# A gated block on one core: the last gate rows of adaLN placed one behind every second weight chunk of both down sweeps

## The chip, the cores and the metric

One of the cores of a Trainium2 chip runs the whole kernel. The metric is the device time of one execution in microseconds (us), as the median of several runs. The engines are named as in the profile: PE is TensorE (matmul), PEld its weight loads, DVE is VectorE, ACT is ScalarE, POOL is GpSimd, SP is SyncE, which here issues the DMAs from one queue, in order. A wait of SP before it issues a DMA is shown under SPq.

## The reference, cut to what matters

One decoder block over 512 tokens of width 2048, in float32. A vector `c` sets six modulation vectors of width 2048 (shift, scale and gate of both sub-layers). The change concerns the last of them, `gt2`, which is the gate of the gated MLP:

```
c_act = silu(c)
mod = c_act @ w_ada + b_ada                 # 2048 -> 6 * 2048
sh1, sc1, gt1, sh2, sc2, gt2 = split(mod, 6)
...
x = x + gt2 * (act @ w_down)                # act: 512 x 5632, w_down: 5632 x 2048
return rmsnorm(x) * norm_f_g
```

## The kernel before, in words

The kernel is one long program for all engines, written in Python and ordered by a scheduler at build time. The scheduler simulates the engines and picks, at each step, the earliest instruction in program order whose operands and buffers are ready in its simulation; the order in which it picks them is the order of each engine's queue. On the chip each engine runs its queue in that order and waits on semaphores. A buffer group (a tag with so many `bufs`) hands out its buffers in turn, so an instruction that fills a buffer waits until the readers of its former content are done.

Activations lie transposed: 128 channels on the partitions, 512 tokens along the row. Each float32 matmul is made as three: weights and activations are split into a high part (`hi`, rounded) and a low part (`lo`, the rest), and `mm3` (lines 120 to 123) issues hi*hi, hi*lo and lo*hi. A weight chunk is 128 x 512 float32, 256 KB, four tiles of 128 x 128. `split_weights` (lines 110 to 118) loads it (`wraw`, 4 buffers), rounds it on ACT (`whi`, 3 buffers, line 115) and subtracts on DVE (`wlo`, 3 buffers, line 117). So one chunk makes 12 matmuls. `project` (lines 125 to 135) runs over the chunks of one output tile.

The last stage is the product with `w_down`, from line 1050 on. The 44 activation tiles were stored to DRAM by the stage before (`actd`). `act_tiles` (lines 1061 to 1067) loads four of them, a slab, through the same four `wraw` buffers (under the name `ald`) and splits each on ACT and DVE (lines 143 and 144). Sweep 1 (lines 1088 to 1101) computes output tiles 0 to 7: 11 slabs, and in each slab one chunk for each of the 8 output tiles, summed up in 8 PSUM banks: 88 chunks. In its last slab `residual` (lines 806 to 809) multiplies each finished bank by its gate, adds it to `x2` and adds the square to `acc`. Sweep 2 (lines 1104 to 1109) does the same for output tiles 8 to 15 over the first 9 slabs: 72 chunks. A tail (lines 1110 to 1126) takes the last two slabs of these tiles in two halves of the tokens, and then normalises and stores the output. The 16 `x2` tiles are loaded at the start of the stage (line 1054).

The gate needs 16 x 128 sums over 2048 products each, and those are made on DVE: `ada_gate2` (lines 1079 to 1085) takes a quarter `kq` of the 2048 inputs, loads that quarter of `c_act` broadcast over the partitions (`cb`, 2 buffers, line 1081), and for each output tile `j` loads a row of weights, 128 x 512 float32, 256 KB (`wa`, 2 buffers, line 1084), and multiplies and sums it in one DVE instruction into `modg` (line 1085). There are 4 x 16 = 64 such rows. They are called in sweep 1, at the head of slabs 1 to 8, eight rows at a time; in slab 9 four small additions on `modg` (lines 1094 to 1097) form the gate `mod[:, 80:96]`, which `gate(f)` (line 1058) hands to the residuals. Nothing ties a row to a place in the sweep but its data, its buffers and its place in program order.

Of the kernel before, what the change touches and what calls it, by code (L numbers as in the profile page):

```python
# [1 line left out]

# [1 line left out]

# [5 lines left out]
F32 = mybir.dt.float32  # L10
# [3 lines left out]
ALU = mybir.AluOpType  # L14
PSUM = bass.MemoryType.PSUM

P = 128
T = 512
D = 2048
KT = D // P  # L20
NF = 44
# [7 lines left out]
NB = 8  # L29
# [5 lines left out]
DK = 4  # L35
# [27 lines left out]
def block_kernel(ctx, tc, a, out, stop=None, dbg=None):  # L63
    nc = tc.nc
    V, S, G, PE = nc.vector, nc.scalar, nc.gpsimd, nc.tensor
# [23 lines left out]
    def cols(name, lo, hi):  # L89
        return vec[:, COLS[name] + lo : COLS[name] + hi]  # L90
# [11 lines left out]
    mod = cp.tile([P, 96], F32, tag="mod", name="mod")  # L102
# [3 lines left out]
    V.tensor_scalar_add(b1p, cols("b_ada", 16, 32), 1.0)  # L106

    mark = [None, None]

    def split_weights(src, eng=V):  # L110
        w = src.shape[-1]
        raw = wp.tile([P, WC], F32, tag="wraw", name="wraw", bufs=4)
        nc.sync.dma_start(raw[:, 0:w], src)
        hi = wp.tile([P, WC], F32R, tag="whi", name="whi", bufs=3)
        mark[0] = S.copy(hi[:, 0:w], raw[:, 0:w]).ins  # L115
        lo = wp.tile([P, WC], F32R, tag="wlo", name="wlo", bufs=3)
        mark[1] = eng.tensor_tensor(lo[:, 0:w], raw[:, 0:w], hi[:, 0:w].bitcast(F32), op=ALU.subtract).ins  # L117
        return hi, lo

    def mm3(ps, wh, wl, xh, xl, start, stop):  # L120
        PE.matmul(ps, wh, xh, start=start, stop=False)  # L121
        PE.matmul(ps, wh, xl, start=False, stop=False)  # L122
        return PE.matmul(ps, wl, xh, start=False, stop=stop)  # L123

    def project(ps, src, acts, start=True, stop=True, engs=(V,)):

        n = len(acts)
        for k0 in range(0, n, WC // P):
            nk = min(WC // P, n - k0)
            wh, wl = split_weights(src[:, k0 * P : (k0 + nk) * P], engs[k0 // 4 % len(engs)])  # L130
            for kk in range(nk):
                k = k0 + kk
                sl = slice(kk * P, (kk + 1) * P)
                last = mm3(ps, wh[:, sl], wl[:, sl], *acts[k], start=start and k == 0, stop=stop and k == n - 1)
        return last

    def slots(k, tag="a"):
        return (actp.tile([P, T], F32R, tag=f"{tag}h{k}", name=f"{tag}h{k}"),
                actp.tile([P, T], F32R, tag=f"{tag}l{k}", name=f"{tag}l{k}"))
# [32 lines left out]
    cact = tc.dram_tile([1, D], F32, name="cact")  # L172
# [6 lines left out]
    if True:  # L179
        cb = p0.tile([P, D], F32, tag="cb", name="cb")  # L180
# [29 lines left out]
        for k in range(KT):  # L210
# [7 lines left out]
            hi, lo = slots(k)  # L218
# [15 lines left out]
        S.copy(rstd, psb)  # L234
        pu.append(pf_bank(7))
        project(pu[7], a["winu7"], H1)
        for i in range(8):
            t = p0.tile([P, T], F32, tag="us", name="us", bufs=2)
# [6 lines left out]
        for k in range(KT):  # L245
# [3 lines left out]
            hi, lo = slots(k)  # L249
# [94 lines left out]
    def win_tile(fi):  # L344
        ps = mmtile()
        project(ps, a["win1"][fi - 8, :, :], H)
        return ps
# [354 lines left out]
    def load_cells(g, names):  # L702
        got = []
        for i in names:
            t = cell(RKV[i], RKV[i].lower())
            for x in range(2):
                nc.sync.dma_start(two(t)[:, x, :], sp[2 * g + x, i])
            got.append(t)
        return got
# [5 lines left out]
    for g in range(NQ):  # L715
# [9 lines left out]
        if g < NQ - 1:  # L725
            win_some(pairs, (0, 2))
            with tc.high_priority(offset=50000):
                r, k = load_cells(g + 1, (0, 1))
# [29 lines left out]
    for f in range(NW):  # L758
        if f % 2 == 0:
            xt = two(cell("K" if f % 4 == 0 else "R", "xt"))  # L760
            nc.sync.dma_start(xt, a["xT"][:, f : f + 2, :])
        ps = mmtile()
        project(ps, a["wout"][f, :, 0 : NM * P], M)
        V.scalar_tensor_tensor(xt[:, f % 2, :], ps, mod[:, 32 + f : 33 + f], xt[:, f % 2, :], op0=ALU.mult, op1=ALU.add)
        d = tc.dram_tile([P, T], F32, name=f"part{f}")
        nc.sync.dma_start(d, xt[:, f % 2, :])
        part.append(d)
# [11 lines left out]
    rb = ctx.enter_context(tc.tile_pool(name="rb", bufs=1, reuse_waits="tile"))  # L779
# [26 lines left out]
    def residual(f, ps, gate, acc, lo, hi, fresh):  # L806

        V.scalar_tensor_tensor(x2[f][:, lo:hi], ps, gate, x2[f][:, lo:hi], op0=ALU.mult, op1=ALU.add)
        sumsq(acc, x2[f][:, lo:hi], lo, hi, fresh)
# [122 lines left out]
    for j in range(2, NORD):  # L932
        tiles = []
        for i in range(2):
            ps = bank()
            last = project(ps, a["wup"][2 * j + i - 4, :, :], H2)
# [78 lines left out]
    for n in range(NST):  # L1015
# [12 lines left out]
        t1, t2, t3, t4 = ([TK[k][i] for k in ks] for i in range(4))  # L1028
# [29 lines left out]
    def gate(f):  # L1058
        return mod[:, 80 + f : 81 + f]

    def act_tiles(k0):
        got = []
        for k in range(k0, k0 + DK):
            t = wp.tile([P, WC], F32, tag="wraw", name="ald", bufs=4)
            nc.sync.dma_start(t, actd[k])
            got.append(split_act(k % KT, t))
        return got

    def down(ps, f, k0, n, acts, start, stop):
        project(ps, a["wdn"][f, :, k0 * P : (k0 + n) * P], acts, start=start, stop=stop)  # L1070
# [5 lines left out]

    modg = cp.tile([P, 4, KT], F32, tag="modg", name="modg")

    def ada_gate2(kq, js):
        cb = rb.tile([P, T], F32, tag="t0", name="cb2", bufs=2)  # L1080
        nc.sync.dma_start(cb, cact[0:1, kq * T : (kq + 1) * T].partition_broadcast(P))
        for j in js:
            wa = rb.tile([P, T], F32, tag="t1", name="wa3", bufs=2)
            nc.sync.dma_start(wa, a["ada3"][kq, j, :, :])
            V.scalar_tensor_tensor(wa, wa, 1.0, cb, op0=ALU.mult, op1=ALU.mult, accum_out=modg[:, kq, j : j + 1])  # L1085

    pss = [bank() for _ in range(NB)]
    for k0 in range(0, NF, DK):
        A = act_tiles(k0)
        n = k0 // DK  # L1090
        if 1 <= n <= 8:
            ada_gate2((n - 1) // 2, range(8 * ((n - 1) % 2), 8 * ((n - 1) % 2) + 8))
        if n == 9:
            V.tensor_add(modg[:, 0, :], modg[:, 0, :], modg[:, 1, :])
            V.tensor_add(modg[:, 2, :], modg[:, 2, :], modg[:, 3, :])
            V.tensor_add(modg[:, 0, :], modg[:, 0, :], modg[:, 2, :])
            V.tensor_add(mod[:, 80:96], modg[:, 0, :], cols("b_ada", 80, 96))
        for f in range(NB):
            down(pss[f], f, k0, DK, A, k0 == 0, k0 + DK == NF)
            if k0 + DK == NF:  # L1100
                residual(f, pss[f], gate(f), acc, 0, T, f == 0)
    pss = [bank() for _ in range(NB)]
    KL = NF - 2 * DK
    for k0 in range(0, KL, DK):
        A = act_tiles(k0)
        for f in range(NB):
            down(pss[f], NB + f, k0, DK, A, k0 == 0, k0 + DK == KL)
            if k0 + DK == KL:
                V.scalar_tensor_tensor(x2[NB + f], pss[f], gate(NB + f), x2[NB + f], op0=ALU.mult, op1=ALU.add)
    A = act_tiles(KL) + act_tiles(KL + DK)  # L1110
    for hf in range(2):
        for n in range(NB):
            f = NB + n
# [121 lines left out]
```

## Time and profile before

| | us |
|---|---|
| median of 3 runs | 2365.94 |
| the three runs | 2362.83, 2365.94, 2372.0 |
| time of the profiled execution | 2367.17 |
| its span, first to last instruction | 2365.4 |
| first matmul of sweep 1 | 1836.8 |
| first and last gate row (starts) | 1860.7, 2004.6 |

All places in time are us from the start of the span. A group's line in the profile gives, after the bar, its busy time, the mean ns of one instruction, and the idle time of the engine just before them with what ended it. A matmul's duration is modelled and overlaps the next one's; where matmuls follow each other without a pause, their starts are 0.227 us apart in this stage. The granted clock of PE (`PEclk`) is 1.00 at full speed.

### The profile page before, as it was taken

How to read it: one execution, taken by the hardware profiler on the slowest of the kernel's cores; microseconds unless marked ns; L12 is line 12 of the kernel's file. 1: busy time of each engine (PE TensorE's matmuls, PEld its weight loads, DVE VectorE, ACT ScalarE, POOL GpSimd, SP SyncE). 2: the span in 40 equal slices, each digit the busy share in tenths (PEclk: the TensorE clock that was granted, in tenths of full speed). 3: DMA queues.
4: the chain of work that ended last, by engine and by line, in shares of the span. 5: the costliest groups of instructions: out<-in, count | busy, mean ns of one | idle time of the engine just before them, and what ended most of it. 6: DMA issues, size and time to landing. Idle time of an engine off the chain costs nothing.

```text
span 2365.4 us, 41904 instructions
## 1 busy us (share of the span) xinstructions
PE 2224.0 (94%) x16306; PEld 1883.8 (80%) x16306; DVE 1512.8 (64%) x2532; ACT 924.0 (39%) x1551; POOL 404.7 (17%) x390
## 2 busy tenths in 40 slices
PE   7998888898979899999999999999999998999997
PEld 5776656665656798889999999999999766888886
DVE  7897667576876469766566666665666555353357
ACT  4335233242423255544434444444444322343333
POOL 0000000000000005643443343433342000000000
PEclk9999999999989999999999999999999999999998
DMA  9885555636775575533333333333334877555555
GB/s 349 301 305 170 157 188 164 205 117 206 226 225 163 179 225 169 148 115 109 116 121 115 113 121 108 116 116 113 109 115 133 272 242 231 148 152 143 143 164 179
DMA packets 197466, 401.42 MB, mean 170 GB/s; under 512 B 37521, under 2 KB 49553, under 8 KB 193041
## 3 DMA queue, kind: packets, MB, share of 16 engines
q1 hardware_dynamic: 197266, 398.73, 53.1%
q8 instruction: 128, 2.10, 0.4%
q14 instruction: 72, 0.59, 0.1%
HBM read 364.56 MB, written 34.09 MB: 169 GB/s over the span
## 4 chain that ended last, share of the span: by engine, by line
PE 48%; DMA 5%; DVE 2%; issue 1%; ACT 0%; SPq 0%; DVEq 0%; ACTq 0%
PE b L123 16%; PE b L121 16%; PE b L122 16%; DMA wa<-ada 2%; DMA ald<-actd 2%; DMA wraw<-wdn 1%; DVE wlo L117 1%; DVE wa L1085 0%; DVE x L1074 0%; DMA x<-x2d 0%; ACT ah L143 0%; DVE al L144 0%; ACT whi L115 0%; SPq L1054 0%; PE b L170 0%
## 5 line engine op out<-in xcount | busy, mean ns | idle before, releaser
L115 ACT CAST whi<-wraw 128x512 fp32r<-128x512 f32 (+1 forms) x594 | 360.1, 609 | 827.8 <-DMA wraw<-wup 264.6
L117 DVE TENSOR_TENSOR wlo<-wraw,whi 128x512 fp32r<-128x512 f32 (+1 forms) x578 | 406.0, 705 | 248.3 <-ACT whi L115 239.9
L123 PE MATMUL b<-ah,wlo 128*128 128x512 f32 (+1 forms) x980 | 352.6, 360 | 16.9 <-DVE wlo L117 15.9
L121 PE MATMUL b<-ah,whi 128*128 128x512 f32 (+1 forms) x980 | 351.3, 358 | 9.4 <-ACT whi L115 8.4
L122 PE MATMUL b<-al,whi 128*128 128x512 f32 (+1 forms) x980 | 349.5, 357 | 0.0
L123 PE MATMUL b<-hh,wlo 128*128 128x512 f32 (+1 forms) x640 | 237.4, 371 | 5.5 <-DVE wlo L117 5.4
L121 PE MATMUL b<-hh,whi 128*128 128x512 f32 (+1 forms) x640 | 237.7, 371 | 0.0
L122 PE MATMUL b<-hl,whi 128*128 128x512 f32 (+1 forms) x640 | 237.2, 371 | 0.0
L123 PEld LDWEIGHTS b<-ah,wlo 128*128 128x128 f32 x980 | 186.6, 190 | 53.2 <-DVE wlo L117 26.6
L121 PEld LDWEIGHTS b<-ah,whi 128*128 128x128 f32 x980 | 186.6, 190 | 38.6 <-ACT whi L115 13.7
L122 PEld LDWEIGHTS b<-al,whi 128*128 128x128 f32 x980 | 186.5, 190 | 26.4
L969 DVE TENSOR_TENSOR pl<-raw,ph 128x768 fp32r<-128x768 f32 x104 | 102.9, 989 | 153.6 <-ACT ph L968 153.6
L123 PE MATMUL mm<-ah,wlo 128*128 128x512 f32 x444 | 186.6, 421 | 6.6 <-DVE wlo L117 6.6
L121 PE MATMUL mm<-ah,whi 128*128 128x512 f32 x444 | 185.5, 418 | 7.2 <-ACT whi L115 6.6
L122 PE MATMUL mm<-al,whi 128*128 128x512 f32 x444 | 183.8, 414 | 0.0
L957 POOL TENSOR_TENSOR sums<-sums,raw 128x256 f32<-128x256 f32 x104 | 107.6, 1034 | 416.1 <-DVE sl L969 410.2
L123 PE MATMUL b<-tk,sl 128*128 128x256 f32 x624 | 176.7, 283 | 0.5 <-DVE sl L969 0.5
L122 PE MATMUL b<-tk,sh 128*128 128x256 f32 x624 | 176.6, 283 | 0.0
L121 PE MATMUL b<-tk,sh 128*128 128x256 f32 x624 | 176.1, 282 | 0.0
L372 DVE SCALAR_TENSOR_TENSOR war<-war,cq 128x1024 f32<-128x1024 f32 x96 | 117.2, 1222 | 85.5 <-DMA war<-ada 85.1
L968 ACT CAST ph<-raw 128x768 fp32r<-128x768 f32 x104 | 86.4, 831 | 164.4 <-PE b L122 157.8
L956 POOL TENSOR_TENSOR sums<-raw 128x512 f32<-128x512 f32 x104 | 137.7, 1324 | 67.9 <-DMA raw<-wups 36.3
(277 smaller groups left out, 4711.1 us busy)
## 6 DMA issues: line engine op xcount, KB each, us to landing
raw<-wups SPq DMA_DIRECT2D x104, 512.0 KB, 3.5
war<-ada SPq DMA_DIRECT2D x96, 512.0 KB, 4.3
wraw<-wdn SPq DMA_DIRECT2D x192, 256.0 KB, 3.1
wraw<-wup SPq DMA_DIRECT2D x160, 256.0 KB, 3.6
wa<-ada SPq DMA_DIRECT2D x32, 1024.0 KB, 7.7
wraw<-win SPq DMA_DIRECT2D x108, 256.0 KB, 4.1
ald<-actd SPq DMA_DIRECT2D x88, 256.0 KB, 2.8
wraw<-wout SPq DMA_DIRECT2D x78, 256.0 KB, 4.0
```

The source lines that it names most:

```text
L115: mark[0] = S.copy(hi[:, 0:w], raw[:, 0:w]).ins
L117: mark[1] = eng.tensor_tensor(lo[:, 0:w], raw[:, 0:w], hi[:, 0:w].bitcast(F32), op=ALU.subtract).ins
L121: PE.matmul(ps, wh, xh, start=start, stop=False)
L122: PE.matmul(ps, wh, xl, start=False, stop=False)
L123: return PE.matmul(ps, wl, xh, start=False, stop=stop)
L372: V.scalar_tensor_tensor(wa, wa, 1.0, cq[0], op0=ALU.mult, op1=ALU.mult, accum_out=modq[:, kq, j : j + 1])
L956: G.tensor_tensor(sa, raw[:, 1:3, :], raw[:, 0:1, :].to_broadcast([P, 2, W2]), op=ALU.add)
L957: G.tensor_tensor(sb2[:, 0, :], sa[:, 0, :], raw[:, 2, :], op=ALU.add)
L968: act = S.copy(hi[:, sl, :], t)
L969: dve = V.tensor_tensor(lo[:, sl, :], t, hi[:, sl, :].bitcast(F32), op=ALU.subtract)
```

## The change

`ada_gate2` becomes a generator. It yields a row when the load of the row after it has been traced too, so that loads are traced one row ahead. Two generators are chained: one makes output tiles 0 to 7 over the four quarters (32 rows), the other tiles 8 to 15 (32 rows); at the seam the second starts its loads only when its first row is asked for. Broadcasts stay at eight in all, rows at 64.

`project` now records the last matmul of each chunk in `beats`. `gate_step(n)` is called after each chunk of both sweeps with the chunk's number, 0 to 87 in sweep 1 and 88 to 159 in sweep 2. On every second chunk from 6 on it takes the next row and gives its DVE instruction an ordering edge behind the last matmul of that chunk (`in_step`). The edge is of the class `NoSync`: the scheduler keeps the order, and no semaphore is waited for on the chip. The loads of rows have no such edge. The first 32 rows end at chunk 68, the last at chunk 132; behind each, four additions half as wide as before form the gate of that half. The first residual that needs a gate comes after chunk 80, the first that needs the second half after chunk 152.

```
+    def in_step(op, beat):
+        tc.add_manual_dep(op.ins, beat.name, mybir.DependencyInfo(mybir.DependencyClass.NoSync,
+                                                                  mybir.DependencyReason.DATA), reason="pace")
...
                 last = mm3(ps, wh[:, sl], wl[:, sl], *acts[k], start=start and k == 0, stop=stop and k == n - 1)
+            beats.append(last.ins)
         return last
...
-    def ada_gate2(kq, js):
-        cb = rb.tile([P, T], F32, tag="t0", name="cb2", bufs=2)
-        nc.sync.dma_start(cb, cact[0:1, kq * T : (kq + 1) * T].partition_broadcast(P))
-        for j in js:
-            wa = rb.tile([P, T], F32, tag="t1", name="wa3", bufs=2)
-            nc.sync.dma_start(wa, a["ada3"][kq, j, :, :])
-            V.scalar_tensor_tensor(wa, wa, 1.0, cb, op0=ALU.mult, op1=ALU.mult, accum_out=modg[:, kq, j : j + 1])
+    def ada_gate2(js):
+        loaded = []
+        for kq in range(4):
+            cb = rb.tile([P, T], F32, tag="t0", name="cb2", bufs=2)
+            nc.sync.dma_start(cb, cact[0:1, kq * T : (kq + 1) * T].partition_broadcast(P))
+            for j in js:
+                wa = rb.tile([P, T], F32, tag="t1", name="wa3", bufs=2)
+                nc.sync.dma_start(wa, a["ada3"][kq, j, :, :])
+                loaded.append((wa, cb, modg[:, kq, j : j + 1]))
+                if len(loaded) == 2:
+                    yield loaded.pop(0)
+        yield loaded.pop(0)
+
+    rows = itertools.chain(ada_gate2(range(NB)), ada_gate2(range(NB, KT)))
+
+    def gate_step(n):
+        if n % 2 or n < 6:
+            return
+        row = next(rows, None)
+        if row:
+            wa, cb, got = row
+            in_step(V.scalar_tensor_tensor(wa, wa, 1.0, cb, op0=ALU.mult, op1=ALU.mult, accum_out=got), beats[-1])
+        done = (n - 4) // 2
+        if done in (4 * NB, 4 * KT):
+            lo = done // 4 - NB
+            r = slice(lo, lo + NB)
+            V.tensor_add(modg[:, 0, r], modg[:, 0, r], modg[:, 1, r])
+            V.tensor_add(modg[:, 2, r], modg[:, 2, r], modg[:, 3, r])
+            V.tensor_add(modg[:, 0, r], modg[:, 0, r], modg[:, 2, r])
+            V.tensor_add(mod[:, 80 + lo : 80 + lo + NB], modg[:, 0, r], cols("b_ada", 80 + lo, 80 + lo + NB))
...
         A = act_tiles(k0)
-        n = k0 // DK
-        if 1 <= n <= 8:
-            ada_gate2((n - 1) // 2, range(8 * ((n - 1) % 2), 8 * ((n - 1) % 2) + 8))
-        if n == 9:
-            V.tensor_add(modg[:, 0, :], modg[:, 0, :], modg[:, 1, :])
-            V.tensor_add(modg[:, 2, :], modg[:, 2, :], modg[:, 3, :])
-            V.tensor_add(modg[:, 0, :], modg[:, 0, :], modg[:, 2, :])
-            V.tensor_add(mod[:, 80:96], modg[:, 0, :], cols("b_ada", 80, 96))
         for f in range(NB):
             down(pss[f], f, k0, DK, A, k0 == 0, k0 + DK == NF)
+            gate_step(k0 // DK * NB + f)
...
             down(pss[f], NB + f, k0, DK, A, k0 == 0, k0 + DK == KL)
+            gate_step((NF + k0) // DK * NB + f)
```

More of the change, by code (lines that the diff above doesn't have):

```diff
@@ L1 @@
 from contextlib import ExitStack
+import itertools
 import numpy as np
@@ L108, in block_kernel @@
     mark = [None, None]
+    beats = []
+    def in_step(op, beat):
+        tc.add_manual_dep(op.ins, beat.name, mybir.DependencyInfo(mybir.DependencyClass.NoSync,
+                                                                  mybir.DependencyReason.DATA), reason="pace")
     def split_weights(src, eng=V):
```

## The prediction

> **What bounds the kernel now.** I read the page first, to see whether TensorE is the limit, and then only the stretch that the edit touches, the two down sweeps: equal amounts of matmul work compared (the windows view), who waited for whom (the waits view), the chain of waits, and single instructions (the timeline).
>
> ```profile
> span 2365.4 us, 41904 instructions
> PE 2224.0 (94%) x16306; PEld 1883.8 (80%) x16306; DVE 1512.8 (64%) x2532; ACT 924.0 (39%) x1551; POOL 404.7 (17%) x390
> ```
>
> PE looks busy nearly everywhere, so gains can only sit in a stage where it stands still. One chunk of weights feeds 12 matmuls. The two stretches below each hold 50 chunks, that is 600 matmuls (the count in brackets has one or two more that straddle an edge). The first is chunks 7 to 56 of sweep 1, with the 64 gate rows; the second is the next 50 chunks, without any row.
>
> ```profile
> core 0: us, PE busy (x) PEld busy (x) DVE busy (x) ACT busy (x) POOL busy (x), PEclk, DMA share, GB/s
> 1860.72:2018.59 157.87, 143.68 (x601) 110.57 (x600) 91.48 (x208) 45.40 (x76) 0.00 (x0) 1.00 0.76 242
> 2018.59:2154.67 136.08, 136.08 (x602) 112.73 (x601) 60.16 (x89) 50.20 (x83) 0.00 (x0) 1.00 0.51 145
> ```
>
> The reader is to see three things. The same work takes 157.87 us with the rows and 136.08 without: **21.8 us are lost while the rows run**, at a full granted clock in both. A clean chunk takes 136.08 / 50 = 2.72 us, and PE is busy for every microsecond of the clean stretch, so 2.72 us is the floor. And the core's DMA engines carry 242 GB/s at a share of 0.76 there, busy but not full.
>
> Only 14.2 us of the loss (157.87 - 143.68) show as PE idle. The Trainium skill ("Perfetto Trace Analysis", Identifying the Most-Contended Engine) says that matmul busy share is a poor measure, since matmuls are pipelined, and wants the LDWEIGHTS share. The rows agree that it understates: matmul busy time alone would make the sum 7.6 us smaller. I go by equal counts of matmuls, which need neither.
>
> Who stopped PE in the first stretch, then what DVE and SP waited for there:
>
> ```profile
> PE b L123 <- DVE wlo L117: 11.5, 15, 1.5
> PE b L121 <- ACT whi L115: 2.5, 4, 1.0
> DVE wa L1085 <- DMA wa<-ada: 45.1, 38, 3.5
> SPq L1084 <- DVE wa L1085: 57.4, 57, 3.1
> SPq L1065 <- DVE mod L1097: 5.0, 1, 5.0
> by line: DMA wa<-ada 36.1%; DMA ald<-actd 21.6%; issue 9.6%; DVE wa L1085 6.9%; DVE wlo L117 5.3%; PE b L123 4.2%; PE b L121 3.6%; PE b L122 3.6%; DMA wraw<-wdn 2.7%; ACT ah L143 2.0%; DVE al L144 1.8%; SPq L1084 0.7%; SPq L113 0.6%; ACT wh
> ```
>
> The last line is the chain of waits for that stretch: it runs through the loads of the rows, not through PE. Columns of the others are total, times, longest. PE waits 19 times, 14.0 us, for a chunk's split. DVE waits 45.1 us for row loads with the splits queued behind; SP waits 57.4 us to issue a row's load until DVE has freed one of two buffers, with weight loads queued behind. One instance:
>
> ```profile
> 1923.25 0.69 DVE L1085 SCALAR_TENSOR_TENSOR wa<-wa,cb 128x512 f32<-128x512 f32 x1 [0.90 <-DMA wa<-ada]
> ...
> 1924.68 0.69 DVE L1085 SCALAR_TENSOR_TENSOR wa<-wa,cb 128x512 f32<-128x512 f32 x1 [0.73 <-DMA wa<-ada]
> ...
> 1925.30 0.69 DVE L117 TENSOR_TENSOR wlo<-wraw,whi 128x512 fp32r<-128x512 f32 x1
> 1926.04 0.50 PE L123 MATMUL b<-ah,wlo 128*128 128x512 f32 x1 [0.62 <-DVE wlo L117]
> ```
>
> Two rows each wait for their load, the split stands behind them, and PE's idle ends when the split does.
>
> **The change, part by part.** *The pace of the rows.* Before, the rows run as fast as two buffers let them:
>
> ```profile
> L1085 DVE SCALAR_TENSOR_TENSOR wa<-wa,cb x64: 681/691/695, 1860.7 to 2004.6; 128x512 f32<-128x512 f32 x64
> L1085 DVE DVE_READ_ACCUMULATOR wa<-wa,cb x64: 78/81/83, 1861.4 to 2005.2; 128x1 f32 x64
> wa<-ada SPq DMA_DIRECT2D x62, 256.0 KB, 3.6
> cb<-cact SPq DMA_DIRECT2D x7, 256.0 KB, 4.7
> ```
>
> 64 rows lie between 1860.7 and 2004.6, one every 143.9 / 63 = 2.28 us. A buffer's round is its load, 3.6 us, and the row, 0.69 + 0.08 = 0.77 us: 4.37 us, and with two buffers one row per 2.19 us. So the rows sit on the latency of their own loads. After, one row stands behind every second chunk: a row per 2 x 2.72 = 5.44 us. Its load can be issued once the row two before it is done, 10.9 us earlier; 3.6 us after that it has landed, some 7 us ahead of need. Neither DVE nor SP should wait for rows, and the 21.8 us go. That the second half of the rows has its buffers traced only at its first row changes little, since a load that waits for nothing but a buffer needs no beat.
>
> *What the rows still cost DVE.* Until row 64 (chunk 132) each chunk pair has a row of 0.77 us more: 14% of 5.44 us on top of 60.16 / 136.08 = 44%. The cover is the lead of the splits over PE in the clean stretch:
>
> ```profile
> 2068.18 0.69 DVE L117 TENSOR_TENSOR wlo<-wraw,whi 128x512 fp32r<-128x512 f32 x1 [2.03 <-ACT whi L115]
> 2072.99 0.39 PE L121 MATMUL b<-ah,whi 128*128 128x512 f32 x1
> ACT whi L115 <- PE b L122: 121.2, 69, 2.1
> ```
>
> The split at 2068.18 is that of the chunk which PE begins at 2072.99: 4.8 us ahead, with 2.03 us of DVE idle before it, because ACT is held by PE (121.2 us over the clean rest of the sweeps): the split buffers are full. A row of 0.77 us fits in the idle and costs nothing; without that cover it would cost 64 x 0.77 = 49 us.
>
> *The stretch where DVE is fullest*, the last slab of sweep 1 with its eight residuals, now gets four rows:
>
> ```profile
> 2083.87:2105.63 21.76, 21.76 (x97) 18.02 (x96) 17.75 (x27) 12.01 (x21) 0.00 (x0) 1.00 0.52 145
> ```
>
> DVE goes from 17.75 to 17.75 + 4 x 0.77 = 20.8 of 21.76 us. It still fits: from nothing to 4 x 0.77 = 3.1 us, and I take nothing, as the row above shows PE without a pause and the lead of 4.8 us stands behind it. Below nothing is out, PE being at its floor.
>
> *SP and the slab starts.* Queued behind a row's load on SP are weight and activation loads. At a slab start the lead is thinnest:
>
> ```profile
> 2051.14 7.21 SPq L113 DMA_DIRECT2D wraw<-wdn  x6
> 2059.39 0.39 PE L121 MATMUL b<-ah,whi 128*128 128x512 f32 x1
> wraw<-wdn SPq DMA_DIRECT2D x98, 256.0 KB, 2.9
> ald<-actd SPq DMA_DIRECT2D x49, 256.0 KB, 2.7
> L115 ACT CAST whi<-wraw 128x512 fp32r<-128x512 f32 (+1 forms) x594 | 360.1, 609 | 827.8 <-DMA wraw<-wup 264.6
> ```
>
> The slab's first weight load leaves at 2051.14, 8.2 us before PE needs it; landing takes 2.9 us, ACT 0.6 and DVE 0.7, which leaves some 4 us. A row's load and a row in between take perhaps 1 us. 16 slab starts have rows about them (chunks 8 to 128). Bounds: nothing (the clean slabs pause nowhere) to the mean pause of before, 14.0 / 19 = 0.74 us, each: 0 to 11.9 us. I take 1.2 us, near the clean rows, because traffic stays under that of before: per slab of 21.8 us twelve loads of 256 KB become 16.5 (four rows, half a broadcast), 145 x 16.5 / 12 = 199 GB/s against 242.
>
> *The start of sweep 1.* The first broadcast and two rows are now traced ahead of slab 1's activations:
>
> ```profile
> 1847.22 1.64 SPq L113 DMA_DIRECT2D wraw<-wdn  x3
> 1849.82 0.33 SPq L1081 DMA_DIRECT2D cb<-cact  x1
> 1853.25 0.50 PE L121 MATMUL b<-ah,whi 128*128 128x512 f32 x1 [2.66 <-ACT whi L115]
> 1836.80:1860.72 23.92, 21.26 (x85) 16.78 (x84) 8.80 (x13) 7.37 (x12) 0.00 (x0) 0.93 0.90 293
> ```
>
> PE idles 2.66 us here for the weights issued at 1847.22, while the x2 tiles load. That pause stays. Three loads of 256 KB ahead of those weights would lengthen it by 0.79 MB / 293 GB/s = 2.7 us; the broadcast away from beside them would shorten it by 0.9 us. I take +0.6, as the weights of chunks 5 and 6 still stand ahead of the rows.
>
> *The small sums.* Four additions become eight of half the width, twice four:
>
> ```profile
> 2005.56 0.17 DVE L1096 TENSOR_TENSOR modg<-modg 128x16 f32<-128x16 f32 x1
> ```
>
> 0.17 us each, in DVE's idle: nothing. The 5.0 us that SP waited behind them lie in the 21.8. Bytes, rows and broadcasts (8) stay as many.
>
> **Sum.** -21.8 + 1.2 + 0.6 = -20.0 us. The profiled execution took 2367.17 us, its span 2365.4 and 1.8 around it; it becomes 2347.2. The median of the three runs, 2365.94, lies 1.2 below it and becomes **2345.9 us**. With all the loss recovered and 0.9 at the start it would be 2343.2.
>
> **The rivals.** *Two buffers still bind.* The Trainium skill ("Perfetto Trace Analysis", Optimization Strategy) reads the same gap repeating on the engine that should be saturated as a sign of too few buffers; by that rule alone the loss would stay, for the change adds none. As a mechanism here: if a row's load leaves less than 3.6 us before its row, because it stands on SP behind weight loads that wait for their own buffers, DVE still waits in front of the splits. Against it: 5.44 us per row is 2.5 times the two-buffer floor of 2.19. If half of the rows meet it, half the loss stays: 2365.9 - 10.9 = 2355.0 us.
>
> *The edge does not hold the rows.* It orders by schedule and adds no wait on the chip; if the scheduler fulfils it early, rows bunch as before: 2365.9 us.
>
> *Slower: SP holds the weights up.* A row's load now waits on SP for a row that stands behind PE-paced splits; everything after it in SP's one queue waits too. Its place is the slab start, with 4 us to spare; from a hold of more than 4 us each row passes it on to PE. Before, a row cost PE 21.8 / 64 = 0.34 us, which is the point of no gain. At the mean pause of 0.74 us per row the loss is 64 x 0.74 = 47.4 us, and the time 2365.9 - 21.8 + 47.4 = 2391.5 us. For it: SP's 57.4 us of such waits now. Against it: the weight load behind waits for the next split anyway, which DVE does right after the row.
>
> **How the numbers follow.** About 0.5% (12 us) is what a measurement of this kernel can tell from no change, so faster means under 2354.1 us. Forecast 0.73; two buffers bind 0.12; the edge does not hold 0.09; SP holds the weights 0.06. Half of the second lies under 2354.1: faster 0.73 + 0.06 = 0.79; same 0.06 + 0.09 = 0.15; slower 0.06. The range runs from 2341 (2343.2, less about 2 us for the run: the fastest of the three lies 3.1 below their median) to 2358, which takes in the second case and the unknown costs at 13.8 instead of 1.8 us, over two thirds of their bounds (11.9 + 2.7 + 3.1 = 17.7); it leaves out the last two cases, 0.15, and a little of the others.
>
> **What would show it.** Right: the sixty-four rows spread over 126 chunks, about 343 us, from near 1858 to near 2200; no DVE wait for row loads worth the name; SP's wait at line 1084 may stay, as nothing behind it is urgent; PE's waits in the sweeps fall from 14.0 us to under 2; 50 chunks from chunk 7 on take 136 to 138 us. Wrong: rows still 2.3 us apart; PE waiting for splits at slab starts; the pause before chunk 5 grown by more than 3 us; PE pauses in sweep 2, which has none now.

## The result, and the profile after

| | before | after |
|---|---|---|
| median of 6 runs each, us | 2367.79 | 2345.81 |
| range of the runs | 2362.83 to 2372.0 | 2339.4 to 2351.19 |
| time of the profiled execution, us | 2367.17 | 2346.13 |
| its span, us | 2365.4 | 2344.4 |
| first matmul of sweep 1 to the end of the span, us | 528.6 | 506.6 |

The ratio of after to before is 0.9903 (95% interval 0.9882 to 0.9925): faster by 22.0 us, or about 1%. In the code after the change the row's product is line 1108, its load 1094, its broadcast 1091; the split of weights is line 124 on DVE and 122 on ACT, the matmuls are lines 128 to 130, the loads of weights 120 and of activations 1073.

First the windows view of the two stretches of 50 chunks that the prediction compared, chunks 7 to 56 and the 50 behind them:

```profile
core 0: us, PE busy (x) PEld busy (x) DVE busy (x) ACT busy (x) POOL busy (x), PEclk, DMA share, GB/s
1861.68:1997.68 136.00, 136.00 (x601) 112.65 (x600) 66.99 (x127) 46.21 (x77) 0.00 (x0) 1.00 0.67 203
1997.68:2133.70 136.02, 136.02 (x602) 112.66 (x601) 75.58 (x143) 50.34 (x83) 0.00 (x0) 1.00 0.66 198
```

The first stretch took 157.87 us before; it takes 136.00, 2.72 us per chunk, and PE is busy through all of it. The second, which had no rows before and has them now, takes 136.02 us against 136.08. So 21.9 us went where the rows had been, and nothing was paid where the rows went. The rows' line (durations in ns, first and last start):

```profile
L1108 DVE SCALAR_TENSOR_TENSOR wa<-wa,cb x64: 682/685/689, 1859.1 to 2204.3; 128x512 f32<-128x512 f32 x64
```

Who waited for whom (total, times, longest): DVE from 1861 to 2230 us, then SP in the first stretch. The same view of PE has no line at all.

```profile
DVE wlo L124 <- ACT whi L122: 146.1, 107, 2.0
DVE al L152 <- ACT ah L151: 29.7, 48, 1.9
DVE x L816 <- PE b L130: 2.4, 2, 1.4
DVE acc L812 <- ACT sqx L811: 1.0, 4, 0.5
```

```profile
SPq L120 <- DVE wlo L124: 37.1, 30, 2.3
...
SPq L1094 <- DVE wa L1108: 5.2, 22, 0.3
```

The rows lie (2204.3 - 1859.1) / 63 = 5.48 us apart, 2.28 before. DVE's 45.1 us of waits for row loads are all gone. SP still waits for row buffers, 22 times in the stretch, but at most 0.3 us at a time. In the timeline of DVE a row now follows a split at once and the next split still comes early:

```profile
1925.22 0.69 DVE L124 TENSOR_TENSOR wlo<-wraw,whi 128x512 fp32r<-128x512 f32 x1 [0.95 <-ACT whi L122]
1925.83 0.68 DVE L1108 SCALAR_TENSOR_TENSOR wa<-wa,cb 128x512 f32<-128x512 f32 x1
1926.44 0.08 DVE L1108 DVE_READ_ACCUMULATOR wa<-wa,cb 128x1 f32 x1
1927.71 0.69 DVE L124 TENSOR_TENSOR wlo<-wraw,whi 128x512 fp32r<-128x512 f32 x1 [1.19 <-ACT whi L122]
```

The split behind the row waits 1.19 us for ACT, so the row sat in time that was idle anyway.

The spans differ by 21.0 us, the stage by 22.0. The difference lies ahead of the change: sweep 1 starts at 1836.8 before and 1837.8 after, and the change does not touch the code up to there. Over all the profiles of this study that start lies between 1832.0 and 1843.4 us, and both ends come from one and the same kernel (the last experiment): a spread of 11.4 us, about as wide as that of the runs of one kernel. So in what follows a kernel is judged by its loss in chunks 7 to 57 (the time of the 50 chunks less 136.1 us, the time of 50 clean ones) and by the time from the first matmul of sweep 1 to the end, and by its total only beside that.

### The profile page after: what moved, and what is told of

Its sections match the earlier page's. It is cut to its first block, busy times and chain, and to the rows that moved or that the text cites. A ratio compares the mean times of both kernels' runs of the same rounds, so it can differ in the third digit from the quotient of the medians.

```text
span 2344.4 us, 41825 instructions
## 1 busy us (share of the span) xinstructions
PE 2214.5 (94%) x16306; PEld 1883.5 (80%) x16306; DVE 1510.3 (64%) x2536; ACT 925.7 (39%) x1551; POOL 405.1 (17%) x390
## 4 chain that ended last, share of the span: by engine, by line
PE 77%; DMA 11%; DVE 8%; issue 2%; ACT 2%; SPq 1%; DVEq 0%; ACTq 0%
PE b L130 20%; PE b L128 20%; PE b L129 20%; DMA war<-ada 5%; PE pf L128 2%; PE mm L130 2%; PE pf L129 2%; PE pf L130 2%; PE mm L128 2%; PE mm L129 2%; DVE war L380 1%; DVE wlo L124 1%; DMA wraw<-wout 1%; DMA wraw<-wdn 1%; DMA sp<-spill 1%
```

## The experiments

The theory: rows that run as fast as two buffers allow make DVE wait for their loads with the splits queued behind, and a slower pace, held by the edge, ends that. Its rivals: the loss was the rows' traffic, or their DVE work, or the lack of buffers, or SP's hold on the weights, or the place in program order is enough without the edge.

**Without any rows.** After, with nothing loaded or multiplied for the gate.

```
-    rows = itertools.chain(ada_gate2(range(NB)), ada_gate2(range(NB, KT)))
+    V.memset(modg[:, :, :], 0.0)
...
-        row = next(rows, None)
+        row = None
```

> The kernel after the change with the 64 gate rows left out: no row is loaded, broadcast or multiplied, the sums are set to zero, so the gate of the MLP is its bias alone. It gives the floor of the two sweeps. Theory (the rows stopped PE only because DVE and SP waited for the rows' own loads, and spread rows cost nothing): chunks 7 to 57 take 136.0 us as in the kernel after, the total lies within 3 us of its 2345.8, and the pause before chunk 5 (2.85 us there) shrinks by at most 0.9 us. Rival (the rows' DVE work and traffic still cost something when they are spread): over 5 us faster than after, under 2340.

Measured: 2344.95 us (2340.88 to 2349.69), ratio to before 0.9919 (0.9894 to 0.9945), where after has 0.9903. The same window of 50 chunks:

```profile
1860.52:1996.52 136.00, 136.00 (x601) 112.61 (x600) 51.87 (x77) 46.15 (x77) 0.00 (x0) 1.00 0.52 150
```

136.00 us, as after has with its rows: DVE works 51.87 us instead of 66.99 and the core moves 150 GB/s instead of 203, and PE's time is the same. From chunk 7 on spread rows are free; the change took everything that the rows had cost there. From the first matmul to the end it is 506.4 us against 506.6, though partly by offsetting differences: chunks 0 to 7 took 1.6 us less, with a clock that did not fall there (see the last section), and the tail behind the sweeps 1.0 us more. The pause before chunk 5 did not shrink (2.70 us, 2.69 in after).

**Without the edge.**

```
-            in_step(V.scalar_tensor_tensor(wa, wa, 1.0, cb, op0=ALU.mult, op1=ALU.mult, accum_out=got), beats[-1])
+            V.scalar_tensor_tensor(wa, wa, 1.0, cb, op0=ALU.mult, op1=ALU.mult, accum_out=got)
```

> The kernel after the change without the ordering edge; the place of each row in program order stays one behind every second chunk. Theory (the edge holds the rows; without it the scheduler moves each row ahead to where its buffer comes free): rows 2.2 to 2.4 us apart as before the change, DVE waits for row loads 35 us or more, chunks 7 to 57 lose 18 to 24 us, total 2362 to 2370. Rival (the place in program order suffices): rows 5.4 us apart, no loss, total about 2346.

Measured: 2364.15 us (2358.56 to 2371.04), ratio 1.0002 (0.9986 to 1.0017): the gain is gone. The rows' line, DVE's wait for row loads in its waits view, and the window of the 50 chunks:

```profile
L1108 DVE SCALAR_TENSOR_TENSOR wa<-wa,cb x64: 681/692/694, 1856.7 to 2006.6; 128x512 f32<-128x512 f32 x64
```

```profile
DVE wa L1108 <- DMA wa<-ada: 45.2, 40, 4.0
```

```profile
1862.43:2016.29 153.86, 143.11 (x601) 110.65 (x600) 90.26 (x206) 45.22 (x77) 0.00 (x0) 1.00 0.78 247
```

The rows are 2.38 us apart again and done by 2006.6, although each stands behind its second chunk in program order. Chunks 7 to 57 lose 17.8 us, a little under the 18 expected and 4.0 less than before the change, by one profile of each; the totals do not differ. So the place in program order alone does little or nothing, and without the edge the rows are not paced.

**A row behind every chunk,** all in sweep 1, two buffers.

```
-        if n % 2 or n < 6:
+        if n < 6:
...
-        done = (n - 4) // 2
+        done = n - 5
```

> The kernel after with a row behind every chunk, not every second, so that all 64 rows end in sweep 1 at chunk 69, still with two buffers. Theory (what counts is a pace slower than the two-buffer floor of 2.19 us per row; here it is 2.72): DVE does not wait for rows, chunks 7 to 57 lose under 3 us, total 2344 to 2350. Rival, traffic: 21 loads of 256 KB per slab, 145 x 21 / 12 = 254 GB/s against 242 before the change, so the loss of 21.8 us stays or grows, total 2366 or more. Rival, two buffers are too few at any pace near this: half the loss or more stays, total 2357 or more.

Measured: 2347.63 us (2345.64 to 2348.68), ratio 0.9927 (0.9902 to 0.9953). The window of the 50 chunks, and DVE's wait for row loads up to the last row; PE again waits nowhere in the sweeps behind 1863 us:

```profile
1863.77:1999.77 136.00, 136.00 (x602) 112.61 (x601) 80.72 (x177) 46.31 (x77) 0.00 (x0) 1.00 0.78 250
```

```profile
DVE wa L1108 <- DMA wa<-ada: 32.2, 23, 3.2
```

No loss, at 250 GB/s, more than the 242 at which before lost 21.8 us. So traffic of this size is not the cause, and two buffers are enough at 2.72 us per row. One part of the theory was too simple: DVE does wait for row loads here, 32.2 us, and PE does not feel it. The splits' lead at the slab starts (from the split's start to the chunk's first matmul) is 0.7 to 2.1 us from slab 4 to slab 9, where it is 4.0 to 4.5 in after, and does not run out. SP, too, still waits 44.3 us here to issue rows' loads (57.4 before the change). So neither wait costs anything by itself: a wait on DVE costs PE only what it takes beyond the lead.

**Two rows behind every chunk,** two buffers: a pace of 1.36 us per row, under the floor.

```
-        row = next(rows, None)
-        if row:
-            wa, cb, got = row
-            in_step(V.scalar_tensor_tensor(wa, wa, 1.0, cb, op0=ALU.mult, op1=ALU.mult, accum_out=got), beats[-1])
-        done = (n - 4) // 2
+        for wa, cb, got in itertools.islice(rows, 2):
+            in_step(V.scalar_tensor_tensor(wa, wa, 1.0, cb, op0=ALU.mult, op1=ALU.mult, accum_out=got), beats[-1])
+        done = 2 * (n - 5)
```

> The kernel after with two rows behind every chunk from chunk 6 on, ordered by edges, two buffers: 1.36 us per row, under the floor of 2.19. Theory: the rows cannot keep that pace, 64 of them take at least 64 x 2.19 = 140 us where their 32 chunks need 87, DVE waits for row loads again (40 us or more), and PE loses between 20 us (as before the change) and 53 us (140 - 87, with every row in front of its splits): total 2364 to 2398. Rival (an edge alone is enough, whatever the pace): loss under 5 us, total 2345 to 2350.

Measured: 2359.4 us in a single run. The rows' line, and the window of the 50 chunks:

```profile
L1106 DVE SCALAR_TENSOR_TENSOR wa<-wa,cb x64: 684/693/696, 1855.4 to 1995.0; 128x512 f32<-128x512 f32 x64
```

```profile
1857.81:2010.79 152.98, 141.56 (x601) 111.10 (x600) 92.07 (x209) 45.93 (x77) 0.00 (x0) 1.00 0.78 248
```

The rows run 139.6 / 63 = 2.22 us apart, at the floor of 2.19 and not at 1.36: an edge sets only how early a row may run. The loss is back, 152.98 - 136.1 = 16.9 us, with 40.7 us of DVE waits, though below the 20 that I had set as its least, as the total lies below the 2364; that the splits would wait behind every row was too much. This window moves 248 GB/s and the one above 250: the same traffic, with 16.9 us of loss and with none.

**More buffers.** The kernel before with four row buffers (two in each of two pools), and the kernel with two rows per chunk with four:

```
-            wa = rb.tile([P, T], F32, tag="t1", name="wa3", bufs=2)
+            wa = (rb, rx)[j % 2].tile([P, T], F32, tag=("t1", "wa4")[j % 2], name="wa3", bufs=2)
```

In the second the generator also runs four loads ahead (`if len(loaded) == 4`, and `yield from loaded` at its end).

> The kernel before the change with four row buffers in place of two, rows in lumps as they were. Theory (a row's pace is its load's latency over the buffers, and rows stop PE when they run at that pace): rows 1.1 to 1.6 us apart instead of 2.28, DVE still waits for row loads, traffic near 300 GB/s while they run, chunks 7 to 57 still lose 8 to 20 us: more buffers alone do not help much. Rival (too few buffers are the cause): loss under 5 us, total under 2350.

> The kernel with two rows behind every chunk (1.36 us per row, which cost 16.9 us with two buffers), now with four buffers, for which latency gives a floor of (3.6 + 0.77) / 4 = 1.09 us per row. Theory: latency no longer binds; what is left is traffic, 30 loads of 256 KB per slab of 21.8 us, 362 GB/s, more than any stretch has shown. At 300 GB/s a slab takes 26.2 us, 4.4 us more for the four slabs: loss 8 to 18 us. If latency were all: loss under 5 us. If buffers do not matter: 17 us, with rows still 2.2 us apart.

Measured, a single run each: lumps with four buffers 2363.35 us, two rows per chunk with four 2356.8. Their stretches of 50 chunks, lumps first, and the second kernel's while its rows run:

```profile
1860.18:2014.51 154.33, 144.30 (x601) 111.79 (x600) 90.80 (x207) 45.27 (x76) 0.00 (x0) 0.99 0.77 248
```

```profile
1858.04:2007.72 149.68, 141.94 (x602) 114.17 (x600) 91.09 (x209) 46.28 (x77) 0.00 (x0) 0.98 0.76 251
1858.04:1957.40 99.36, 91.62 (x380) 72.49 (x378) 70.50 (x176) 29.23 (x48) 0.00 (x0) 0.97 0.86 297
```

With lumps the loss is 18.2 us against 21.8: the rows come faster (1.90 us apart, not the 1.1 to 1.6 expected, and at 271 GB/s while they run, not near 300), and DVE still waits 32.2 us for them. The gain from the buffers is small, and by one profile each it is not even certain: the kernel without the edge lost 17.8 us with two buffers. With two rows per chunk DVE's waits for row loads nearly go (6.0 us; rows 1.67 us apart), yet 13.6 us are lost. The core moves 297 GB/s while the rows run, against 242 to 250 in the stretches above, and PE then waits for the rounding of weights on ACT and no longer for splits, and ACT 22.4 us for the loads of these weights. PE stops four times there, 7.6 us in all, and the mean granted clock is 0.97, so part of the loss is a slower clock behind the stops (see the last section). That fits traffic as the next limit, as expected, but this run does not part it from other causes.

**The rows' loads on POOL's queue.** The kernel before, and SP freed of the loads of rows; the eight broadcasts stay on SP.

```
-            nc.sync.dma_start(wa, a["ada3"][kq, j, :, :])
+            nc.gpsimd.dma_start(wa, a["ada3"][kq, j, :, :])
```

> The kernel before the change with the rows' loads issued from the queue of POOL, which has no other work in this stage, in place of SP's; the rows stay in lumps on DVE. It parts the two ways in which a row can hold up a chunk. If the weights come late because SP holds them behind a row's load: the loss of 21.8 us falls under 6. If the splits come late because DVE holds them behind a row that waits for its load: DVE still waits 35 us or more for row loads and the loss stays between 14 and 24 us. I take the second for likelier, 0.6 to 0.4.

Measured: 2382.47 us in a single run, the slowest of all. The window of the 50 chunks, and one line each of DVE's and PE's waits in it:

```profile
1857.79:2031.96 174.17, 148.47 (x601) 112.49 (x600) 90.74 (x204) 45.37 (x76) 32.18 (x60) 0.98 0.70 220
```

```profile
DVE wa L1085 <- DMA wa<-ada: 59.6, 44, 4.4
```

```profile
PE b L123 <- DVE wlo L117: 22.5, 18, 2.0
```

With less traffic (220 GB/s) and no row load on SP the loss rises to 38.1 us, beyond the 14 to 24 expected, and DVE's wait for row loads rises with it, to 59.6 us. A row's load that stands on SP ahead of the weights is not needed for the loss: it follows DVE's waits. What SP's part was in the kernel before this run does not show, since on POOL's queue the rows also get later (2.52 us apart).

The trace of the kernel before shows it for most of the loss. PE stopped 15 times for a split while the rows ran, 11.5 us in all. Each time the chunk's weights had been rounded 1.4 to 7.1 us before the split began, and each time DVE came to the split straight from rows (once with the small sums in between), 14 times after a wait for a row's load. In the instance that the prediction shows, the split began at 1925.30 and the weights had been rounded by 1919.17:

```profile
1918.55 0.62 ACT L115 CAST whi<-wraw 128x512 fp32r<-128x512 f32 x1 [2.14 <-PE b L122]
```

So in these stops the weights were not late; DVE held the split up. A hold on SP can stand at most behind the other four stops, which were for the rounding on ACT: 2.5 of 14.0 us.

**The x2 loads moved.** The pause before chunk 5, which the change left alone, is now the only one in the sweeps. After, with the 16 x2 loads spread by the same edge:

```
     for f in range(KT):
         t = rx.tile([P, T], F32, tag=f"x2_{f}", name=f"x2_{f}")
-        nc.sync.dma_start(t, x2d[f])
         x2.append(t)
...
     def gate_step(n):
+        if n % 4 == 3 and 11 <= n < 75:
+            f = (n - 11) // 4
+            in_step(nc.sync.dma_start(x2[f], x2d[f]), beats[-1])
```

> The kernel after, and the 16 loads of the x2 tiles moved from the start of the stage into sweep 1, one behind every fourth chunk from 11 to 71, with the same kind of edge. Theory (the pause before chunk 5 is made by the 16 x2 loads that stand on SP ahead of that chunk's weights): the pause of 2.85 us and the slow matmuls behind it go, chunks 0 to 7 lose under 1 us in place of 4.9, no new loss later (18.5 loads per slab, under the 21 of the kernel with a row behind every chunk), total 2339 to 2343. Rival (the pause has another cause, the stores of the last activations on SP): chunks 0 to 7 still lose 3 us or more, total 2344 or more.

Measured: 2343.56 us (2338.58 to 2346.58), ratio 0.9915 (0.9897 to 0.9933). The pause is gone (chunks 0 to 7 lose nothing, 4.9 in after), and from the first matmul to the end it takes 501.4 us. But sweep 1 began at 1843.4 in the profile, and the total was above the band. So both kernels ran once more, side by side:

> The kernel after once more, beside the next one on the same chip. Theory (the place where sweep 1 starts wobbles by up to 10 us from run to run in code that the change does not touch, and the change takes 22 us from the stage behind it): from the first matmul of sweep 1 to the end 506 to 507 us, as in its first profile (506.6), whatever the total; total 2341 to 2350.

> The kernel with the x2 loads moved once more, beside the kernel after. Its first profile had no pause before chunk 5 and 501.4 us from the first matmul of sweep 1 to the end, but a sweep 1 that started 5.7 us later, and no shorter total. Theory (that late start was the wobble upstream): 501 to 502 us again, the start back within 1833 to 1841, and a median 3 to 7 us under that of the kernel after. Rival (moving the loads delays the stage before): sweep 1 starts at 1842 or later again, and the medians lie within 2 us.

Measured: after 2343.33 us (2339.29 to 2345.9), ratio 0.9914 (0.9891 to 0.9937); with the x2 loads moved 2338.45 us (2334.92 to 2340.58), ratio 0.9893 (0.987 to 0.9915). From chunk 0 to chunk 7 in the two, after first:

```profile
1835.90:1859.66 23.76, 21.20 (x85) 16.74 (x84) 8.65 (x14) 6.80 (x12) 0.00 (x0) 0.93 0.91 310
```

```profile
1832.01:1851.05 19.04, 19.04 (x86) 15.77 (x84) 10.21 (x16) 7.95 (x14) 0.00 (x0) 1.00 0.74 228
```

19.04 us is seven chunks of 2.72. From the first matmul to the end it is 505.4 us in after (1 under what was expected) and 501.6 here. Sweep 1 started at 1832.0, even a little ahead of the 1833 to 1841 expected, so moving the loads does not make it start late. The medians differ by 4.9 us, about the 4.7 that chunks 0 to 7 lose in after (23.76 less 19.04). In its stage this version beats the kernel after in both pairs of profiles (501.4 against 506.6, 501.6 against 505.4). The totals alone do not settle it: the intervals of the two ratios overlap, and in its first runs its ratio was no better than that of after.

## Why the prediction was right

The predicted median was 2345.9 us; 2345.81 was measured. That is closer than the method can claim, with runs of one kernel some 10 us apart, and it is luck: the forecast gain of 20.0 us was 2.0 too small, but it was taken off the median of the first three runs, 2365.94, and that of six runs is 2367.79, 1.85 higher. The steps are the better test.

- *The loss of 21.8 us while the rows run, all of it theirs.* Right: 21.9 us went, and the kernel without rows is no faster from chunk 7 on. The count of equal matmuls was the right measure: PE's idle time of 14.2 us would have forecast two thirds of it, which agrees with what the Trainium skill ("Perfetto Trace Analysis", Identifying the Most-Contended Engine) says of matmul busy share.
- *The pace and the two-buffer floor.* Right, and shown from both sides: 2.72 us per row costs nothing, 1.36 us asked for gives 2.22 and a loss of 16.9. No pace between 2.19 and 2.72 was set.
- *DVE's idle time covers the rows.* Right; the fullest slab went from 17.75 to about 18.8 us of DVE work and not to 20.8, since three rows and not four fell into it and 1.0 us of other work moved out of it, and the lead held.
- *The slab starts, +1.2 us.* Too dear: no pause at any of them. *The start of sweep 1, +0.6 us.* Too dear: chunks 0 to 7 lose 4.8 us before the change and 4.9 after it. So the sum should have been 21.8 us; the stage gave 22.0, and in the profiled execution a start 0.9 us later left 21.0 of it.
- *The rivals.* The edge does hold the rows, and without it the gain is nothing, as that rival had priced it. SP still waits for row buffers, 15.8 us in 58 waits over both sweeps where it was 57.4, and holds nothing up. The Trainium skill ("Perfetto Trace Analysis", Optimization Strategy) says that repeated gaps can mean too few buffers. Here the measurement decides otherwise: four buffers with the rows in lumps won back at most 3.6 of 21.8 us, pace with two buffers all of it.

One sentence of it was too strong, that neither DVE nor SP should wait for rows if the gain is to come: with a row per chunk DVE waits 32.2 us and nothing is lost.

## What to carry to other kernels

Small side work on an engine that also feeds the bottleneck should be paced slower than the round of its own loads over its buffers (here 2.19 us; a pace of 2.72 was enough). Where a scheduler fills queues by readiness, as here, an ordering edge paces it, and the place in program order does not. Measure such a loss by equal amounts of the bottleneck's work in a stretch with and one without the side work, and look at what is in front of it in the waiting engine's queue: a wait of DVE costs only what exceeds the lead of the work behind it.

## What the runs showed of the hardware that was not expected

Behind the pause before chunk 5, PE's granted clock fell to 0.67 over 5.2 us in after (a pause of 2.69 us), but stayed at 1.00 behind the same pause (2.70 us) in the kernel without rows, whose chunks 0 to 7 took 1.6 us less. After first:

```profile
1854.20:1859.40 5.20, 5.18 (x15) 3.83 (x16) 2.87 (x5) 2.57 (x5) 0.00 (x0) 0.67 0.96 339
```

```profile
1854.60:1859.80 5.20, 5.12 (x21) 3.97 (x22) 3.31 (x5) 2.90 (x6) 0.00 (x0) 1.00 0.61 193
```

The first row counts 15 matmuls in 5.2 us and the second 21. The length of the pause alone does not decide it: over the sweeps of all these traces the clock fell behind pauses of 1.63 us (rows' loads on POOL's queue), 2.15 and 2.28 us (two rows per chunk, four buffers), and stayed at 1.00 behind others of 2.38 us (no edge), 2.39 us (two rows per chunk, four buffers) and the 2.70 us above. What else decides it is left open; the pause itself is the thing to remove.

By the traces, an issue of a load on POOL's queue takes 0.54 us (0.33 on SP's), and DVE waited longer for the rows' loads from there, so an idle queue was no cheap way out here.
